# A transformer layer on one core: three top-k searches go from VectorE to ScalarE, one goes to a later stage, and tile start addresses are evened out

## The chip, the cores and the metric

The program runs on one core of a Trainium2 chip (trn2). The metric is device microseconds of one execution. A core has five instruction queues, each issued in order: TensorE (PE in the profile; its weight loads have a row of their own, PEld), VectorE (DVE), ScalarE (ACT), GpSimd (POOL) and SyncE (SP), which here only starts DMA transfers. All working data lie in SBUF, an on-chip memory with 128 partitions; matrix products go to PSUM. Tile sizes below are given as partitions x elements.

## The reference

One layer over 2048 tokens of width 1024, all in float32, then a final normalisation:

```
h   = RMSNorm(x);  P = h @ W_in              # split into conv inputs, q, k, v, iq, ik, iw, gates
y_a = (B * causal_conv3(C * x_a)) @ W_a
score[t,s] = sum_h iw[t,h] * relu(iq[t,h] . ik[s])    # causal, 8 index heads
keep the 256 best s of each t; softmax attention over these (8 heads, one k and v), bias by distance
y_b = attn @ W_b
x   = x + (sigmoid(g_a) * y_a + sigmoid(g_b) * y_b) @ W_out
x   = x + (silu(h2 @ W_g) * (h2 @ W_u)) @ W_d,   h2 = RMSNorm(x)
out = RMSNorm(x)
```

The choice of the 256 best must be exact, ties included. Queries are handled in 16 blocks of 128 (block 0 to 15). Blocks 0 and 1 have no more than 256 keys and need no choice, so a threshold is searched for in blocks 2 to 15. Block b has (b+1)*128 keys.

## The kernel before

**Arithmetic.** Each float32 product is made of three matmuls in the fp32r type: both operands are split into a rounded part (`hi`, written by ScalarE, line 129) and the rest (`lo`, line 130), and `mm3` (lines 155 to 157) multiplies hi by hi, hi by lo and lo by hi. A matmul has a stationary operand, 128x128, loaded ahead of it, and a moving operand of up to 512 columns.

**Stages.** The first stage forms all projections of h (lines 489 to 553). Between its matmuls, one in three, `proj` takes a step of `scores`: `score(b)` multiplies the index heads of a block with the keys (lines 258, 259, tile `sc`), ScalarE takes the relu (261, tile `r`), VectorE weights and sums (266, tile `acc`), and the finished scores go to memory (`SD`). When a block is scored, its threshold is searched. Then come two halves, each of eight blocks: attention (`attention(half)`, blocks 7 to 0, then 15 to 8), the mixer (branch products, gates, W_out, RMSNorm and transposes of h2), and the feed-forward layer (FFN, from line 889 on), with tiles `wgu` (gate and up weights), `h2hi`/`h2lo`, `hid` and `wd`. Half 0 attends to blocks 0 to 7 and needs their masks alone; half 1 needs those of blocks 8 to 15.

**The search.** Two versions give the same threshold. `descend(b)` on VectorE counts in each of 32 passes how many keys reach a trial value (line 285, tile `J`) and corrects the trial value by small instructions on 128x1 tiles (316 to 341). `descend_act(b)` makes integer keys on VectorE (381 to 384), then ScalarE does the 33 passes: a Sign over all keys with a running sum (358, tile `dump`, with a read of the accumulator), and two small instructions (367, 369, tiles `way` and `nt`). In the middle VectorE takes ScalarE's result (393, `top<-nt`) and makes new keys (400, 401); at the end it takes the second result (410, `li<-nt`). After either, `topk` (425 to 448) turns scores and threshold into a mask of 0 and -1e30 on VectorE and SP writes it to memory (`MS`). The tables `A_ACT`, `A_DVE` and `C_ACT` say which block is searched where: before, blocks 2, 3, 4 by VectorE and 5 to 10 by ScalarE in the first stage; 15, 14, 13, 12, 11 by ScalarE after half 0's attention, in its mixer and FFN. One search runs at a time, since the search tiles have one buffer each.

**What sets the order.** Each engine's queue is fixed when the program is built. A scheduler puts instructions into it by data dependencies, priority and its own estimate of when operands are ready; searches have the lowest priority (`tc.high_priority(offset=-LOW)`), so they fill what the scheduler takes for gaps. On the chip a queue goes in order: if an instruction waits, all behind it on that engine wait. `tc.issue_after(ins)` puts the instructions of its block that are on the engine of `ins` behind it in the queue (an order, not a wait). `ends[-1]` is VectorE's last `pl` of attention (line 680), `transposed[-1]` its last `h2lo` (line 150) of the mixer.

**Where tiles start.** SBUF is handed out in pools, from the left end or (`side="right"`) from the right end, one after the other, each tile rounded up to 32 bytes; so the size of a small tile shifts what lies beyond it. The built program gives these start addresses, modulo 512 bytes, of matmul operands before:

| product (output <- moving, stationary) | moving | stationary |
|---|---|---|
| first stage: `mm`, `sc` | 320 | 320 |
| attention logits `lg` | 320 | 320 |
| attention transposes `tpb<-ident,pr` | 128 | 192 |
| attention values `pv<-ph,V` and `pv<-pl,V` | 192 | 320 |
| mixer, `gu<-y,wab`, half 0 / half 1 | 320 / 448 | 320 / 448 |
| mixer, `gu<-o,wab`, half 0 / half 1 | 320 / 320 | 320 / 448 |
| W_out, `dn<-mg,o` | 320 | 320 |
| FFN gate and up, `gu<-h2,wgu`, half 0 / half 1 | 320 / 320 | 320 / 448 |
| FFN down, `dn<-hid,wd` | 320 | 320 |

Of the kernel before, what the change touches and what calls it, by code (L numbers as in the profile page):

```python
# [12 lines left out]
F32 = mybir.dt.float32  # L13
# [12 lines left out]
P = 128  # L26
# [4 lines left out]
CH = 512  # L31
# [15 lines left out]

A_ACT, A_DVE = (5, 6, 7, 8, 9, 10), (2, 3, 4)
C_ACT, C_DVE = (15, 14, 13, 12, 11), ()
ORDER = ((7, 6, 5, 4, 3, 2, 1, 0), (15, 14, 13, 12, 11, 10, 9, 8))  # L50
# [24 lines left out]
def trunk_kernel(tc, x, g_mix, w_in, b_gate, conv_w, w_a, w_b, w_out, rel_bias,  # L75
# [38 lines left out]
    bg = const.tile([P, 16], F32, name="bg")  # L114
    zero = edge.tile([P, 1], F32, name="zero")
    nc.gpsimd.memset(zero, 0.0)
# [133 lines left out]
    def score(b):  # L250
# [3 lines left out]
        for s0, w in cut((b + 1) * P):  # L254
            acc = tk.tile([P, CH], F32, name="acc", tag="acc", bufs=2)
            for h in range(NH):
                sc = scp.tile([P, CH], F32, name="sc", tag="sc")
                nc.tensor.matmul(sc[:, 0:w], iqb[:, h, :], IKH[:, s0:s0 + w], start=True, stop=False)
                nc.tensor.matmul(sc[:, 0:w], iqb[:, h, :], IKL[:, s0:s0 + w], start=False, stop=True)
                r = tk.tile([P, CH], F32, name="r", tag="r", bufs=3)  # L260
                nc.scalar.activation(r[:, 0:w], sc[:, 0:w], AF.Relu)  # L261
# [29 lines left out]
    def parts(b):  # L291

        for s0, w in cut((b + 1) * P):
            S = TK["p"].tile([P, CH], F32, name="S", tag="S", bufs=2)
            nc.sync.dma_start(out=S[:, 0:w], in_=SD[b][:, s0:s0 + w])
            yield slice(s0, s0 + w), w, S[:, 0:w].bitcast(U16).rearrange("p (n e) -> p n e", e=2)

# [155 lines left out]

    def select_block_act(b):
        with tc.high_priority(offset=-LOW):
            thr = descend_act(b)
            topk(b, thr, TK["a"].tile([P, TK["alen"]], U8, name="dump", tag="dump", bufs=1).bitcast(BF16))

# [100 lines left out]
    def attention(half):  # L559
# [3 lines left out]
        ap = pool(b_stack, f"ap{half}")  # L563
        prp = pool(b_stack, f"pr{half}")
        lgp = pool(b_stack, f"lg{half}", bufs=LGB, space=PSUM)
        tpb = pool(b_stack, f"tpb{half}", bufs=7 - LGB, space=PSUM)
# [47 lines left out]
        def logits(st, hg, res):  # L614

            b, n, q, Mt, spans, near, MBs = st
            lw = spans[-1][1]
            sums = ap.tile([P, 4], F32, name="sums", tag="sums", bufs=3)
            for hh in range(4):
# [3 lines left out]
                pr = prp.tile([P, LH], F32, name="pr", tag="pr", bufs=PRB[half])  # L623
                mx = ap.tile([P, 5], F32, name="mx", tag="mx", bufs=6)
                for i, (s0, w) in enumerate(spans):
# [12 lines left out]
                yield  # L638
            rec = ap.tile([P, 4], F32, name="rec", tag="rec", bufs=3)
            nc.vector.reciprocal(rec, sums)  # L640
            res.append(rec)

        def spread(b, hg, rec):

            tp = tpb.tile([P, CH], F32, name="tpb", tag="tpb")
            in_order(nc.tensor.transpose(tp[0:4, 0:P], rec, ident))
            row = ap.tile([4, P], F32, name="row", tag="row", bufs=2)
            nc.scalar.copy(row, tp[0:4, 0:P])
            rd = RD[2 * b + hg]
            nc.sync.dma_start(out=rd, in_=row)  # L650
            R = ap.tile([P, CH], F32, name="R", tag="R", bufs=3)
            nc.sync.dma_start(out=R, in_=bass.AP(rd[:].tensor, rd[:].offset, [[0, P], [1, CH]]))
            return R
# [90 lines left out]
    for half in (0, 1):  # L744
        ends = attention(half)
        mc = ExitStack()
        if half == 0:
            search_pool(mc, "tkc", C_DVE, C_ACT, 4)
            TK["p"].tile([P, 16], F32, name="pad")
        bigp = pool(mc, f"bigp{half}", bufs=4)  # L750
# [119 lines left out]
        if half == 0:  # L870
            with tc.issue_after(ends[-1].ins):
                for b, ba in itertools.zip_longest(C_DVE, C_ACT):
                    if ba is not None:
                        select_block_act(ba)
                    if b is not None:
                        select_block(b)
        if half == 1:
# [104 lines left out]
```

## Time and profile before

| | |
|---|---|
| median of 3 runs | 3313.43 us (3310.44 to 3317.68) |
| the profiled execution | 3308.23 us, span 3306.3 us |
| granted TensorE clock, mean | 0.99 |
| first stage | to about 1004 us |
| half 0: attention, mixer, FFN | to about 1140, 1360 and 2072 us |
| half 1: attention, mixer, FFN | to about 2390, 2576 and 3297 us |

The profile is of one execution. "x" is a count of instructions; a stretch "A:B" is in us from the start of the span. Recorded matmuls overlap, since their ends are modelled: a matmul of 512 columns is recorded with some 390 ns, while the next starts about 227 ns later, so for speed the count in a stretch says more than the mean duration. The number in brackets behind a row of the timeline is the time that the engine stood idle before it and what ended that.

### The profile page before, as it was taken

To read this page: it belongs to the slowest core of one execution; us is meant where nothing else is said; L and a number is where in the kernel's file an instruction comes from. 1 tells how busy PE (TensorE), PEld (TensorE's weight loads), DVE (VectorE), ACT (ScalarE), POOL (GpSimd) and SP (SyncE) were. 2 spreads that over 40 slices of the span, in tenths; PEclk is the share of its full clock that TensorE was granted. 3 is DMA by queue.
4 is the path that set the end of the run, shared out by engine and by line. 5 is a ranking of instruction groups with operands and counts; after the bars stand their busy time and mean duration, and the time that the engine had idled before them with its cause. 6 is when DMAs were issued, how large, how long until landed. Compare 5 with 4: busy or idle time off the path is not lost.

```text
span 3306.3 us, 41232 instructions
## 1 busy us (share of the span) xinstructions
PE 3206.5 (97%) x14723; PEld 2626.5 (79%) x14723; DVE 1744.3 (53%) x3422; ACT 1763.8 (53%) x3250; POOL 774.4 (23%) x684
## 2 busy tenths in 40 slices
PE   8999899999997899899999999999999999999999
PEld 6777788888886678788888888787787888888887
DVE  6389756565327775554535423898854422332234
ACT  6433478877877786867586611677632211111111
POOL 5411012221013520321221222222222222212221
PEclk9999999999999999999999999999999999999999
DMA  7643333333235692322212211422571411111111
GB/s 231 179 126 115 93 97 96 92 98 107 85 99 137 167 287 78 98 78 83 88 60 77 79 51 60 115 60 72 149 250 45 147 51 44 46 51 45 45 45 51
DMA packets 347077, 328.94 MB, mean 99 GB/s; under 512 B 20596, under 2 KB 276808, under 8 KB 346488
## 3 DMA queue, kind: packets, MB, share of 16 engines
q1 hardware_dynamic: 310248, 297.84, 29.4%
q0 software_dynamic: 36624, 28.48, 4.0%
q8 instruction: 115, 1.88, 0.2%
q14 instruction: 90, 0.74, 0.1%
HBM read 252.28 MB, written 75.54 MB: 99 GB/s over the span
## 4 chain that ended last, share of the span: by engine, by line
PE 79%; DVE 9%; DMA 5%; ACT 3%; issue 2%; POOL 1%; SPq 0%; POOLq 0%; DVEq 0%; ACTq 0%
PE gu L155 11%; PE gu L157 11%; PE gu L156 11%; PE mm L157 6%; PE mm L155 6%; PE mm L156 6%; PE dn L155 5%; PE dn L157 5%; PE dn L156 5%; PE tpb L676 3%; DVE J L285 2%; PE pv L663 2%; PE lg L629 1%; PE pv L664 1%; PE lg L630 1%
## 5 line engine op out<-in xcount | busy, mean ns | idle before, releaser
L155 PE MATMUL gu<-h2hi,wgu 128*128 128x512 f32 x1408 | 552.7, 393 | 0.0
L156 PE MATMUL gu<-h2lo,wgu 128*128 128x512 f32 x1408 | 552.1, 392 | 0.0
L157 PE MATMUL gu<-h2hi,wgu 128*128 128x512 f32 x1408 | 552.0, 392 | 0.0
L358 ACT ACTIVATE dump<-key,nt 128x768 uint8<-128x768 int16 (+21 forms) x330 | 484.2, 1467 | 8.4
L157 PE MATMUL mm<-hThi,wlo 128*128 128x512 f32 (+2 forms) x1216 | 471.7, 389 | 2.6 <-POOL wlo L130 2.5
L155 PE MATMUL mm<-hThi,whi 128*128 128x512 f32 (+2 forms) x1216 | 473.7, 390 | 0.4 <-ACT whi L129 0.4
L156 PE MATMUL mm<-hTlo,whi 128*128 128x512 f32 (+2 forms) x1216 | 471.1, 388 | 0.0
L937 DVE SCALAR_TENSOR_TENSOR x<-dn,x 128x512 f32<-128x512 f32 x352 | 241.7, 689 | 224.4 <-PE dn L157 224.3
L130 POOL TENSOR_TENSOR wlo<-raw,whi 128x512 fp32r<-128x512 f32 (+1 forms) x132 | 175.9, 1333 | 696.8 <-ACT whi L129 659.3
L156 PEld LDWEIGHTS gu<-h2lo,wgu 128*128 128x128 f32 x1408 | 265.2, 188 | 58.5
L157 PEld LDWEIGHTS gu<-h2hi,wgu 128*128 128x128 f32 x1408 | 265.0, 188 | 58.6
L155 PEld LDWEIGHTS gu<-h2hi,wgu 128*128 128x128 f32 x1408 | 265.2, 188 | 58.4
L130 POOL TENSOR_TENSOR hid<-th,hid 128x512 fp32r<-128x512 f32 x88 | 114.6, 1302 | 808.1 <-ACT hid L129 800.8
L266 DVE SCALAR_TENSOR_TENSOR acc<-r,iwT,acc 128x512 f32<-128x512 f32 (+2 forms) x266 | 196.1, 737 | 197.3 <-ACT r L261 196.6
L920 DVE SCALAR_TENSOR_TENSOR th<-th,gu 128x512 f32<-128x512 f32 x88 | 60.5, 687 | 432.5 <-ACT th L919 379.0
L130 POOL TENSOR_TENSOR wgu<-raw,wgu 128x1024 fp32r<-128x1024 f32 x88 | 216.6, 2462 | 271.5 <-ACT wgu L129 268.4
L155 PE MATMUL dn<-wd,hid 128*128 128x512 f32 x704 | 274.5, 390 | 0.0
L157 PE MATMUL dn<-wd,hid 128*128 128x512 f32 x704 | 274.1, 390 | 0.0
L156 PE MATMUL dn<-wd,hid 128*128 128x512 f32 x704 | 274.0, 389 | 0.0
L157 PEld LDWEIGHTS mm<-hThi,wlo 128*128 128x128 f32 (+1 forms) x1216 | 227.1, 187 | 54.5 <-POOL wlo L130 5.1
L155 PEld LDWEIGHTS mm<-hThi,whi 128*128 128x128 f32 (+1 forms) x1216 | 227.4, 187 | 44.1 <-ACT whi L129 1.7
L156 PEld LDWEIGHTS mm<-hTlo,whi 128*128 128x128 f32 (+1 forms) x1216 | 227.4, 187 | 42.9
(229 smaller groups left out, 5853.3 us busy)
## 6 DMA issues: line engine op xcount, KB each, us to landing
raw<-in_w_in_dram SPq DMA_DIRECT2D x124, 256.0 KB
raw<-in_w_ffn_gate_dram SPq DMA_DIRECT2D x44, 512.0 KB
raw<-in_w_ffn_up_dram SPq DMA_DIRECT2D x44, 512.0 KB
raw<-in_w_ffn_down_dram SPq DMA_DIRECT2D x44, 512.0 KB
S<-SD SPq DMA_DIRECT2D x80, 256.0 KB
GT<-f SPq DMA_DIRECT2D x64, 256.0 KB
ta<-GT SPq DMA_DIRECT2D x64, 256.0 KB
S<-SD SPq DMA_DIRECT2D x68, 192.0 KB
```

What stands on the lines that cost most here:

```text
L130: lo_eng.tensor_tensor(lo, raw, hi.bitcast(F32), op=ALU.subtract)
L155: nc.tensor.matmul(ps, whi, xhi, start=start, stop=False)
L156: nc.tensor.matmul(ps, whi, xlo, start=False, stop=False)
L157: nc.tensor.matmul(ps, wlo, xhi, start=False, stop=stop)
L266: nc.vector.scalar_tensor_tensor(acc[:, 0:w], r[:, 0:w], wv, acc[:, 0:w], op0=ALU.mult, op1=ALU.add)
L285: nc.vector.tensor_scalar(wide("J")[:, 0:n], xs, thr, None, op0=op, op1=ALU.add, accum_out=cnt)
L358: nc.scalar.activation(dump, keys, AF.Sign, bias=nt, accum_out=sm)
L629: in_order(nc.tensor.matmul(lg[:, o2:e2], q[:, h, :], KH[:, s0 + o2:s0 + e2], start=True, stop=False))
L663: in_order(nc.tensor.matmul(pv, V[:, sb, :], ph, start=sb == 0, stop=False))
L676: in_order(nc.tensor.transpose(tp[:, hh * P:(hh + 1) * P], Ps[hh][:, sb * P:(sb + 1) * P], ident))
L920: nc.vector.scalar_tensor_tensor(th, th, 1.0, g, op0=ALU.add, op1=ALU.mult)
L937: nc.vector.scalar_tensor_tensor(x2[tt][:, ns], ps, 0.5, x2[tt][:, ns], op0=ALU.mult, op1=ALU.add)
```

## The change

Four things are altered. Blocks 2 to 9 are searched by ScalarE in the first stage and none by VectorE; blocks 15 to 10 by ScalarE after half 0's attention, so block 10 moves from the first stage to there. Of these, only block 15's passes may start in the mixer: its `topk`, and all that VectorE does for blocks 14 to 10, is queued behind the last `h2lo`. Some buffers grow: `r` from 3 to 4, `S` (scores read back) from 2 to 4 in the second group. And tile sizes are set so that pools start elsewhere: `zero` takes 160 bytes instead of 4, the pad in the second search pool 448 instead of 64, and four small attention tiles go to a pool of their own (`few`).

```
-A_ACT, A_DVE = (5, 6, 7, 8, 9, 10), (2, 3, 4)
-C_ACT, C_DVE = (15, 14, 13, 12, 11), ()
+A_ACT, A_DVE = tuple(range(2, 10)), ()
+C_ACT, C_DVE = (15, 14, 13, 12, 11, 10), ()
...
-    zero = edge.tile([P, 1], F32, name="zero")
+    zero = edge.tile([P, 40], F32, name="zero")[:, 0:1]
...
-                r = tk.tile([P, CH], F32, name="r", tag="r", bufs=3)
+                r = tk.tile([P, CH], F32, name="r", tag="r", bufs=4)
...
-            S = TK["p"].tile([P, CH], F32, name="S", tag="S", bufs=2)
+            S = TK["p"].tile([P, CH], F32, name="S", tag="S", bufs=TK["eqs"])
...
-    def select_block_act(b):
-        with tc.high_priority(offset=-LOW):
+    def select_block_act(b, after=()):
+        with tc.high_priority(offset=-LOW), ExitStack() as stack:
             thr = descend_act(b)
+            for ins in after:
+                stack.enter_context(tc.issue_after(ins))
             topk(b, thr, TK["a"].tile([P, TK["alen"]], U8, name="dump", tag="dump", bufs=1).bitcast(BF16))
...
         prp = pool(b_stack, f"pr{half}")
+        few = pool(b_stack, f"few{half}")
...
-            sums = ap.tile([P, 4], F32, name="sums", tag="sums", bufs=3)
+            sums = few.tile([P, 4], F32, name="sums", tag="sums", bufs=3)
...
-            TK["p"].tile([P, 16], F32, name="pad")
+            TK["p"].tile([P, 112], F32, name="pad")
...
             with tc.issue_after(ends[-1].ins):
-                for b, ba in itertools.zip_longest(C_DVE, C_ACT):
-                    if ba is not None:
-                        select_block_act(ba)
-                    if b is not None:
-                        select_block(b)
+                select_block_act(C_ACT[0], [transposed[-1].ins])
+            with tc.issue_after(transposed[-1].ins):
+                for b in C_ACT[1:]:
+                    select_block_act(b)
```

The tiles `mx`, `rec` and `row` move to `few` in the same way as `sums`. In the built program after the change every operand of the table above starts at 320 modulo 512, but for `ident`, which stays at 128; the transposes so have 128 and 320.

The change moves instructions in the queues. Three places, all on VectorE, follow, each as it stood and as it stands now (line numbers past 297 are up to three higher after the change).

In the first stage, where block 2's search begins. `acc<-r` is the summing of scores, `f<-mm` (line 228) takes a projection out of PSUM, `J` is a counting pass. Before:

```order
L266 SCALAR_TENSOR_TENSOR acc<-r,iwT,acc 128x512
L316 TENSOR_SCALAR drop<-cnt 128x1
L318 SCALAR_TENSOR_TENSOR c<-c,drop 128x1
L228 SCALAR_TENSOR_TENSOR f_2222<-mm,f_2222 64x512
L285 TENSOR_SCALAR J,cnt<-up,c 128x384
L316 TENSOR_SCALAR drop<-cnt 128x1
L318 SCALAR_TENSOR_TENSOR c<-c,drop 128x1
L266 SCALAR_TENSOR_TENSOR acc<-r,iwT,acc 128x512
```

After:

```order
L266 SCALAR_TENSOR_TENSOR acc<-r,iwT,acc 128x512
L381 TENSOR_SCALAR key<-S 128x384
L382 TENSOR_SCALAR dump<-S 128x384
L384 SCALAR_TENSOR_TENSOR key<-dump,key 128x384
L266 SCALAR_TENSOR_TENSOR acc<-r,iwT,acc 128x512
L228 SCALAR_TENSOR_TENSOR f_2197<-mm,f_2197 64x512
L266 SCALAR_TENSOR_TENSOR acc<-r,iwT,acc 128x512
L228 SCALAR_TENSOR_TENSOR f_2201<-mm,f_2201 64x512
```

The counting passes and their small instructions are gone from VectorE; three instructions that make the keys stand there once.

At the opening of half 0's attention. `pr,mx<-lg` (line 632, 635 after the change) takes logits out of PSUM; the profile calls it CUSTOM_DVE_ANT_0. Before:

```order
L401 SCALAR_TENSOR_TENSOR key<-S,base,dump 128x384
L410 TENSOR_SCALAR li<-nt 128x1
L413 TENSOR_TENSOR li<-li,turn 128x1
L415 TENSOR_TENSOR thr<-li,top 128x1
L425 SCALAR_TENSOR_TENSOR dump,cnt_7133<-S,thr,zerob 128x512 x2
L632 ISA pr,mx<-lg,Mt 128x512
L632 ISA mx 128x1
L431 TENSOR_TENSOR more<-cnt_7133 128x1
L632 ISA pr,mx<-lg,Mt 128x512
```

After:

```order
L446 SCALAR_TENSOR_TENSOR eq<-S,thr,eq 128x384
L447 TENSOR_SCALAR eq<-eq 128x384
L635 ISA pr,mx<-lg,Mt 128x512
L635 ISA mx 128x1
L635 ISA pr,mx<-lg,Mt 128x512
L635 ISA mx 128x1
L635 ISA pr,mx<-lg,MB,mx 128x512
```

Before, the end of block 10's search and its `topk` stand ahead of and among the first logits; now the first stage's last search, of block 9, ends ahead of them with its `topk`, and no search instruction stands among them.

At the end of half 0's mixer. `x<-dn` adds a W_out product, `o<-x` is the norm, `h2lo` the rest of a transposed tile that the FFN reads. Before:

```order
L150 TENSOR_TENSOR h2lo<-gu,h2hi 128x4x128
L381 TENSOR_SCALAR key<-S 128x512
L382 TENSOR_SCALAR dump<-S 128x512
L150 TENSOR_TENSOR h2lo<-gu,h2hi 128x4x128
L381 TENSOR_SCALAR key<-S 128x512
L384 SCALAR_TENSOR_TENSOR key<-dump,key 128x512
L140 SCALAR_TENSOR_TENSOR o_13632<-x_12890,rs,gB 128x1024
L382 TENSOR_SCALAR dump<-S 128x512
L381 TENSOR_SCALAR key<-S 128x384
L864 SCALAR_TENSOR_TENSOR x_12988<-dn,x_12988 128x512
```

After:

```order
L150 TENSOR_TENSOR h2lo<-gu,h2hi 128x4x128 x2
L140 SCALAR_TENSOR_TENSOR o_13264<-x_12522,rs,gB 128x1024
L867 SCALAR_TENSOR_TENSOR x_12620<-dn,x_12620 128x512
L150 TENSOR_TENSOR h2lo<-gu,h2hi 128x4x128 x2
L140 SCALAR_TENSOR_TENSOR o_13286<-x_12571,rs,gB 128x1024
L140 SCALAR_TENSOR_TENSOR o_13308<-x_12620,rs,gB 128x1024
L867 SCALAR_TENSOR_TENSOR x_12669<-dn,x_12669 128x512
L150 TENSOR_TENSOR h2lo<-gu,h2hi 128x4x128 x2
L140 SCALAR_TENSOR_TENSOR o_13330<-x_12669,rs,gB 128x1024
L150 TENSOR_TENSOR h2lo<-gu,h2hi 128x4x128 x8
L425 SCALAR_TENSOR_TENSOR dump,cnt_13610<-S,thr,zerob 128x512
```

Before, the key making of block 14 stands among the norms and transposes; now the search's next VectorE work, block 15's `topk`, stands behind the last `h2lo`.

More of the change, by code (lines that the diff above doesn't have):

```diff
@@ L623, in logits @@
                 pr = prp.tile([P, LH], F32, name="pr", tag="pr", bufs=PRB[half])
-                mx = ap.tile([P, 5], F32, name="mx", tag="mx", bufs=6)
+                mx = few.tile([P, 5], F32, name="mx", tag="mx", bufs=6)
                 for i, (s0, w) in enumerate(spans):
@@ L638, in logits @@
                 yield
-            rec = ap.tile([P, 4], F32, name="rec", tag="rec", bufs=3)
+            rec = few.tile([P, 4], F32, name="rec", tag="rec", bufs=3)
             nc.vector.reciprocal(rec, sums)
@@ L646, in spread @@
             in_order(nc.tensor.transpose(tp[0:4, 0:P], rec, ident))
-            row = ap.tile([4, P], F32, name="row", tag="row", bufs=2)
+            row = few.tile([4, P], F32, name="row", tag="row", bufs=2)
             nc.scalar.copy(row, tp[0:4, 0:P])
```

## The prediction

> **What bounds the kernel now.** I read the page first, then a table of stretches, then the waits and the timeline of the stretches that lose time. The page's busy line and its chain of waits:
>
> ```profile
> PE 3206.5 (97%) x14723; PEld 2626.5 (79%) x14723; DVE 1744.3 (53%) x3422; ACT 1763.8 (53%) x3250; POOL 774.4 (23%) x684
> ...
> PE 79%; DVE 9%; DMA 5%; ACT 3%; issue 2%; POOL 1%; SPq 0%; POOLq 0%; DVEq 0%; ACTq 0%
> ```
>
> TensorE sets the end. No matmul is removed, so time can come from two sources only: PE's idle stretches, and the pace of its matmuls. Busy time by stretch (length, busy us and count of each engine, granted clock, DMA) shows both:
>
> ```profile
> core 0: us, PE busy (x) PEld busy (x) DVE busy (x) ACT busy (x) POOL busy (x), PEclk, DMA share, GB/s
> 180.00:400.00 220.00, 204.42 (x890) 163.84 (x889) 198.53 (x583) 75.92 (x154) 26.00 (x21) 0.98 0.40 116
> 400.00:1004.00 604.00, 603.38 (x2694) 502.58 (x2694) 298.32 (x555) 496.79 (x1111) 105.75 (x88) 1.00 0.35 100
> 404.00:465.00 61.00, 61.00 (x278) 51.20 (x277) 21.67 (x43) 57.54 (x148) 8.75 (x7) 1.00 0.29 82
> ...
> 1004.00:1052.00 48.00, 32.21 (x153) 22.74 (x151) 38.30 (x101) 32.69 (x60) 15.56 (x22) 0.89 0.39 108
> ...
> 1320.00:1360.00 40.00, 30.23 (x149) 25.10 (x148) 32.94 (x48) 25.88 (x45) 13.84 (x15) 0.83 0.47 146
> 1400.00:2040.00 640.00, 640.00 (x2825) 529.90 (x2824) 278.39 (x500) 364.22 (x603) 143.01 (x77) 1.00 0.22 68
> 1890.00:2070.00 180.00, 180.00 (x795) 149.03 (x795) 53.89 (x77) 26.74 (x36) 44.17 (x31) 1.00 0.21 67
> 2072.00:2110.00 38.00, 35.81 (x167) 24.68 (x167) 34.82 (x87) 24.03 (x32) 8.15 (x13) 1.00 0.59 144
> 2536.00:2576.00 40.00, 36.37 (x176) 30.05 (x175) 27.28 (x31) 22.50 (x38) 17.24 (x19) 0.91 0.40 127
> 2600.00:3240.00 640.00, 640.00 (x2771) 521.07 (x2770) 187.73 (x259) 106.43 (x139) 142.76 (x82) 1.00 0.16 50
> ```
>
> Three stretches lose time while a search is on: 180:400 (VectorE 90% busy), 1004:1052 and 1320:1360. For the last two, half 1 has the same stage without a search (2072:2110, 2536:2576). And the two FFNs, the same 3168 matmuls each, run at different paces with PE busy throughout.
>
> **180:400, VectorE's own searches go.** What they cost VectorE there by group, and then, from the waits (us, times, longest), what PE waited for:
>
> ```profile
> L285 DVE TENSOR_SCALAR_CACHE_REDUCE J<-up,l 128x384 bf16<-128x384 uint16 (+2 forms) x48 | 35.8, 745 | 1.4
> L285 DVE TENSOR_SCALAR_CACHE_REDUCE J<-up,c 128x384 bf16<-128x384 bf16 (+2 forms) x45 | 33.5, 745 | 1.3
> L341 DVE SCALAR_TENSOR_TENSOR l<-l,ldrop 128x1 f32<-128x1 f32 x48 | 11.3, 235 | 1.4
> ```
>
> ```profile
> PE sc L258 <- ACT r L261: 13.2, 11, 6.5
> ```
>
> The counts and the three other small groups beside L341 (each of 45 to 48 instructions) took roughly 100 us of VectorE. With them gone the sums of scores no longer queue, `r` comes free and ScalarE can empty `sc`, which is what PE waited for. The loss by count: 400:1004 holds 2694 matmuls in 604 us, 0.2242 each, with a like mix; 890 would take 199.5, so 20.5 us are lost in 220. By PE's busy time it is 15.6, since a modelled end hides part of a gap.
>
> The searches move to ScalarE. One pass costs a Sign, a read and two small instructions:
>
> ```profile
> L358 ACT ACTIVATE dump<-key,nt 128x768 uint8<-128x768 int16 x15 | 14.0, 934 | 0.4
> L358 ACT ACTIVATE dump<-key,nt 128x1408 uint8<-128x1408 int16 x15 | 22.0, 1468 | 0.4
> L358 ACT ACTIVATE dump<-key,nt 128x2048 uint8<-128x2048 int16 x15 | 30.0, 1997 | 0.3
> L358 ACT ACTIVATION_READ_ACCUMULATOR dump<-key,nt 128x1 f32 x330 | 61.8, 187 | 0.0
> L367 ACT ACTIVATE way<-sm,over 128x1 f32<-128x1 f32 x176 | 50.7, 288 | 2.6
> L367 ACT ACTIVATE way<-sm 128x1 f32<-128x1 f32 x176 | 34.2, 195 | 2.1
> L369 ACT ACTIVATE nt<-way,nt 128x1 f32<-128x1 f32 x330 | 96.5, 292 | 8.2
> ```
>
> Block 5 (768 keys): 33 x (0.934 + 0.187) + 16 x (0.288 + 0.195) + 32 x 0.292 = 54 us. Block 10 (1408): 72. The slope is 3.5 us per 128 keys, so blocks 2, 3, 4 come to an estimated 44, 47 and 51: ScalarE gains 142 us in the first stage and loses block 10's 72 there. What hides it: 404:465 lies inside block 5's search and has ScalarE 94% busy, PE 100%, VectorE 36%. ScalarE's own work in 180:400 is 75.92/220, 35%, and the search takes the rest as it comes. I take 19 of the 20.5 us; below it could be 10, if the shorter, more frequent passes make `r` late, above 21.
>
> The eight searches still end in time: block 10's own 72 us, the longest of the six of before, were done at 1012.75 (below). Now the longest is block 9's, 128 keys shorter, the first can start as soon as block 2 is scored, and in the queue block 9's `topk` stands ahead of the first logits.
>
> **1004:1052, block 10 leaves.** The timeline:
>
> ```profile
> 1005.71 0.39 PE L630 MATMUL lg<-KL,q 128*128 128x512 f32 x1
> ...
> 1012.75 0.15 DVE L410 TENSOR_SCALAR li<-nt 128x1 int32<-128x1 f32 x1 [39.84 <-ACT nt L369]
> ...
> 1014.79 0.69 DVE L632 CUSTOM_DVE_ANT_0 pr<-lg,Mt 128x512 f32<-128x512 f32 x1
> ...
> 1015.54 0.80 PE L629 MATMUL lg<-KH,q 128*128 128x512 f32 x1 [9.44 <-DVE mx L632]
> ```
>
> VectorE's queue stood at L410 for ScalarE's last pass; the first L632 was behind it and three PSUM tiles were full. Then `topk` shared VectorE with the logits until 1052. PE idles 48 - 32.21 = 15.8; half 1's opening idles 38 - 35.81 = 2.2, so 2.8 in 48. Gain 13; by count, 153 matmuls at 2072:2110's 167 in 38 need 34.8 of 48, again 13. Bounds: 9.4, the one stall, and 15.8, all idle time.
>
> Block 10's 72 us go behind block 11. What hides them: in 1890:2070 ScalarE is busy 26.74 of 180 us. The passes of the kernel before by their line (first and last start, us), and the first mask load of half 1 in GpSimd's timeline:
>
> ```profile
> L358 ACT ACTIVATION_READ_ACCUMULATOR dump<-key,nt x330: 185/187/201, 396.0 to 1873.0; 128x1 f32 x165
> ```
>
> ```profile
> 2056.50 0.55 POOL L600 DMA_DIRECT2D Mt<-MS  x1
> ```
>
> The search ended at about 1873. An estimated 20 us of `topk` and 100 to 120 for block 10 (its 72 us among ScalarE's other work, 15% there, and waits for VectorE at two points) put its mask near 2010, and it is the sixth block of half 1. Nothing. Without that cover, half 1 would wait for the excess.
>
> **1320:1360, the mixer's end.** The wait there (us, times, longest), VectorE's queue, and the same wait in 2536:2576:
>
> ```profile
> PE gu L147 <- DVE h2lo L150: 9.8, 4, 5.6
> ```
>
> ```profile
> 1339.34 2.60 DVE L382 TENSOR_SCALAR dump<-S 128x512 bf16<-128x512 bf16 x1
> ...
> 1343.33 1.27 DVE L150 TENSOR_TENSOR h2lo<-gu,h2hi 128x512 fp32r<-128x512 f32 x2
> ```
>
> ```profile
> PE gu L147 <- DVE h2lo L150: 3.6, 4, 1.2
> ```
>
> Key making stood ahead of `h2lo`, and now does not. 9.8 against 3.6: 6 us, as 149 against 176 matmuls in 40 us say too (27 x 0.227). Bounds 2 and 7. What is late next: block 15's `topk` falls into the FFN's first 20 us. Four PSUM tiles hold PE's first 22 us of FFN output, so I price it at nothing.
>
> **A price.** Block 15's passes now begin after the mixer's second `wab` split, before after the seventh. Each is 2.0 us and what is behind it waits, while PE starts on few weights. I take 2 us; bounds 0 and 10 (five passes).
>
> **The addresses.** Per 512-column matmul, half 0's FFN takes 640/2825 = 226.5 ns, half 1's 640/2771 = 231.0. The groups in these two stretches, half 0 first:
>
> ```profile
> L155 PE MATMUL gu<-h2hi,wgu 128*128 128x512 f32 x622 | 242.0, 389 | 0.0
> L157 PE MATMUL dn<-wd,hid 128*128 128x512 f32 x320 | 124.5, 389 | 0.0
> ```
>
> ```profile
> L155 PE MATMUL gu<-h2hi,wgu 128*128 128x512 f32 x604 | 238.5, 395 | 0.0
> L157 PE MATMUL dn<-wd,hid 128*128 128x512 f32 x320 | 125.2, 391 | 0.0
> ```
>
> The product whose stationary operand starts at 448 and moving one at 320 is the slow one; `dn`, 320 and 320 in both, is nearly even. ScalarE, VectorE and DMA are all less busy in half 1, so neighbours do not explain it. With all at 320 half 1 should run at 226.5: 3168 x 4.5 ns = 14 us. Bounds 0 and 15 (a little in `gu<-o,wab`). In attention the transposes' `ident` stays at 128, so I expect nothing, at best 3 us.
>
> The Trainium skill says otherwise. Its page "TensorE: Matmul & The Clock Gate" (Part 2, Step-by-step) gives PE two independent read ports and states "Loading the next tile's weights doesn't steal SBUF read bandwidth from the running matmul". By that rule the start addresses change nothing and this term is 0. The two paces above speak against it, though they do not prove the cause.
>
> **Sum.** -19 - 13 - 6 + 2 - 14 = -50 on the profiled execution's 3308.2: 3258. The runs' median, 3313.4, lies 5 higher, and the result will be a median too: 3263. Its own range: -21 - 16 - 7 - 18 = -62 to -10 - 9 - 2 + 10 = -11, so 3251 to 3302.
>
> **Rivals.** *Addresses do nothing* (13%): 3263 + 14 = 3277. For it, half 1's FFN differs in other ways too, such as the final norms of half 0 that it carries; against it, gate and up differ and down hardly.
>
> *ScalarE takes VectorE's place as limit in 180:400* (10%): PE waits for `r` all the same, and the 19 us stay: 3282. For it, 94% busy in a search and more `f` evacuations at 180:400 than later; against it, 0.62 us idle in 604 beside six such searches.
>
> *VectorE's queue stands for ScalarE's results* (7%): what happened at 1012.75 repeats. There are now 16 such points in the first stage (393 and 410 for eight blocks), with `acc` and `f` behind them. Each that holds PE for 9.4 us takes that back; from the sixth on (56 us) the kernel is slower than before, 3319, with eight 3338. Against it: ten such points in 400:1004 cost PE 0.62 us together. That the change does not do what it says is ruled out by the queues and the start addresses shown.
>
> **How the numbers follow.** The forecast holds 65%, the rivals 30, a larger gain (attention too, or stalls of 1100:1160) 5. The time is 3263. 3242 to 3294 holds the forecast's own range but its end, the first two rivals and half of the larger gains. A measurement of this kernel tells some 0.2%, 7 us. Slower: the third rival, 7%. Within 0.2%: the second and first together with poor other terms, 5%. Faster: 88%.
>
> **What would show it.** Right: in the stretch after block 2 is scored, PE 99% busy and `PE sc <- ACT r` under 3 us; no L410 ahead of the first logits and PE idle under 5 us in their first 48; the same `gu <- h2lo` wait near 3.6; half 1's FFN at 226.5 ns a matmul. Wrong: 231 ns there (first rival); long idle times before L393 or L410 with PE idle at the same time (third); ScalarE at 99% with PE waiting for `r` (second).

## The result and the profile after

| | before | after |
|---|---|---|
| median | 3313.57 us (4 runs, 3310.44 to 3317.68) | 3264.53 us (4 runs, 3260.28 to 3265.59) |
| ratio | | 0.9849, 95% interval 0.9832 to 0.9866 |
| profiled execution, span | 3306.3 us | 3262.3 us |

The kernel became 49 us faster by the medians and 44.0 by the two profiled spans; 3263 was forecast. The page of after, its busy line and the shares of its chain:

```profile
PE 3184.9 (98%) x14723; PEld 2623.9 (80%) x14723; DVE 1667.0 (51%) x3046; ACT 1886.7 (58%) x3646; POOL 780.3 (24%) x684
...
PE 71%; ACT 11%; DMA 6%; DVE 6%; issue 4%; POOL 2%; SPq 0%; POOLq 0%; ACTq 0%; DVEq 0%
```

TensorE still sets the end; ScalarE's share of the chain has grown from 3 to 11%. The stretches of the prediction, at their new places (length, busy us and count of each engine, granted clock, DMA):

```profile
core 0: us, PE busy (x) PEld busy (x) DVE busy (x) ACT busy (x) POOL busy (x), PEclk, DMA share, GB/s
180.00:400.00 220.00, 220.00 (x999) 184.51 (x998) 96.37 (x192) 192.91 (x537) 27.70 (x23) 1.00 0.40 119
980.00:1028.00 48.00, 45.07 (x248) 34.95 (x247) 42.14 (x115) 38.92 (x76) 21.46 (x32) 1.00 0.38 104
...
1290.00:1330.00 40.00, 37.56 (x190) 30.72 (x189) 33.17 (x52) 18.80 (x31) 14.07 (x14) 1.00 0.37 116
1400.00:2030.00 630.00, 624.66 (x2742) 515.07 (x2742) 295.62 (x529) 425.76 (x724) 148.00 (x84) 1.00 0.25 76
...
2560.00:3200.00 640.00, 640.00 (x2825) 530.01 (x2824) 190.99 (x262) 107.92 (x142) 147.05 (x87) 1.00 0.18 54
```

First row: 999 matmuls where 890 stood, and PE never idle. Second: the 48 us around attention's opening have PE idle for 2.9 us instead of 15.8. In the second and third row the granted clock is 1.00, where it was 0.89 and 0.83. Last: 640/2825 = 226.5 ns a matmul in half 1's FFN. The row that nobody forecast is 1400:2030: in half 0's FFN PE, which had been without a gap, now idles 5.3 us, and 2742 matmuls stand where 630 us at 226.5 ns would hold 2781, 8.9 us fewer.

For the comparison of runs the program is cut by the starts of the first matmul of each stage in the trace (first `lg` of a half for attention, first `gu` from `wgu` for the FFN; the first stage begins with the program's first matmul, the last ends with its last). Lengths in us:

| stage | before | after | difference | forecast |
|---|---|---|---|---|
| first stage | 996.7 | 973.0 | -23.7 | -19 |
| half 0, attention and mixer | 353.4 | 330.7 | -22.7 | -13 - 6 + 2 = -17 |
| half 0, FFN | 707.5 | 718.5 | +11.0 | 0 |
| half 1, attention and mixer | 499.2 | 505.0 | +5.8 | 0 |
| half 1, FFN | 733.1 | 718.7 | -14.4 | -14 |
| sum | | | -44.0 | -50 |

The new loss shows in PE's waits in half 0's FFN of after (us, times, longest); before, this list is empty:

```profile
PE dn L155 <- ACT hid L129: 3.1, 2, 1.9
PE dn L157 <- POOL hid L130: 1.9, 3, 0.6
PE dn L155 <- DVE x L939: 0.9, 1, 0.9
PE dn L155 <- DVE base L397: 0.9, 1, 0.9
```

One of these places, followed back from PE. PE's timeline of after, then ScalarE's and VectorE's ahead of it:

```profile
1488.71 0.39 PE L157 MATMUL dn<-wd,hid 128*128 128x512 f32 x1
1490.96 0.50 PE L155 MATMUL dn<-wd,hid 128*128 128x512 f32 x1 [1.87 <-ACT hid L129]
```

```profile
1486.03 1.79 ACT L358 ACTIVATE dump<-key,nt 128x1792 uint8<-128x1792 int16 x1
...
1488.51 1.79 ACT L358 ACTIVATE dump<-key,nt 128x1792 uint8<-128x1792 int16 x1
...
1490.30 0.61 ACT L129 ACTIVATE hid<-th 128x512 fp32r<-128x512 f32 x1
```

```profile
1478.05 0.60 DVE L445 SCALAR_TENSOR_TENSOR eq<-cs,need,eq 128x384 bf16<-128x384 f16 x1
1478.57 0.68 DVE L923 TENSOR_TENSOR th<-gu,th 128x512 f32<-128x512 f32 x1
1479.17 0.68 DVE L384 SCALAR_TENSOR_TENSOR key<-dump,key 128x512 int16<-128x512 bf16 x1
...
1482.96 0.56 DVE L384 SCALAR_TENSOR_TENSOR key<-dump,key 128x384 int16<-128x384 bf16 x1
1483.44 0.68 DVE L922 SCALAR_TENSOR_TENSOR th<-th,gu 128x512 f32<-128x512 f32 x1
1484.22 0.69 DVE L923 TENSOR_TENSOR th<-gu,th 128x512 f32<-128x512 f32 x1
```

Block 14's `topk` and block 13's keys stand among the gate and up products: between the L923 of one 512-column unit and the L922 of the next VectorE ends that `topk` and makes keys for 4 us. The next unit's `th` is done at 1484.91, and then ScalarE has passes of block 13 (1792 keys) queued ahead of `hid`, which starts 5.4 us later. The down product needs that very `hid`. Before, block 14's `topk` stood among the down products, where its pieces lie between the `x` (L937) and no `th` waits:

```profile
1475.59 0.67 DVE L937 SCALAR_TENSOR_TENSOR x<-dn,x 128x512 f32<-128x512 f32 x1
1476.17 0.14 DVE L444 CAST last<-cs 128x1 f32<-128x1 f16 x1
1476.23 0.74 DVE L445 SCALAR_TENSOR_TENSOR eq<-cs,need,eq 128x512 bf16<-128x512 f16 x1
1476.89 0.48 DVE L441 TENSOR_SCALAR eq<-S,thr 128x512 bf16<-128x512 f32 x1
1477.28 0.74 DVE L446 SCALAR_TENSOR_TENSOR eq<-S,thr,eq 128x512 bf16<-128x512 f32 x1
1477.94 0.68 DVE L937 SCALAR_TENSOR_TENSOR x<-dn,x 128x512 f32<-128x512 f32 x1
```

### The profile page after: what moved, and what is told of

It is laid out like the page before. It is cut to its first block, busy times and chain, and to the rows that moved or that the text cites. A ratio compares the mean times of both kernels' runs of the same rounds, so it can differ in the third digit from the quotient of the medians.

```text
span 3262.3 us, 41287 instructions
## 1 busy us (share of the span) xinstructions
PE 3184.9 (98%) x14723; PEld 2623.9 (80%) x14723; DVE 1667.0 (51%) x3046; ACT 1886.7 (58%) x3646; POOL 780.3 (24%) x684
## 4 chain that ended last, share of the span: by engine, by line
PE 71%; ACT 11%; DMA 6%; DVE 6%; issue 4%; POOL 2%; SPq 0%; POOLq 0%; ACTq 0%; DVEq 0%
PE mm L155 8%; PE mm L157 8%; PE mm L156 8%; PE gu L157 7%; PE gu L155 7%; PE gu L156 7%; ACT dump L358 6%; PE dn L155 4%; PE dn L157 4%; PE dn L156 4%; PE tpb L679 3%; PE sc L259 2%; PE sc L258 2%; PE pv L666 2%; PE pv L667 2%
## 5 line engine op out<-in xcount | busy, mean ns | idle before, releaser
L358 ACT ACTIVATE dump<-key,nt 128x384 uint8<-128x384 int16 (+27 forms) x420 | 549.0, 1307 | 10.7
L922 DVE SCALAR_TENSOR_TENSOR th<-th,gu 128x512 f32<-128x512 f32 x88 | 60.3, 685 | 391.9 <-ACT th L921 355.2
```

The lines of the kernel that those rows point to most:

```text
L358: nc.scalar.activation(dump, keys, AF.Sign, bias=nt, accum_out=sm)
```

## The experiments

All stage lengths below are taken from the traces as in the table above. "before" in a comparison is the kernel before on the same chip.

| run | median us | first stage | half 0 att.+mixer | half 0 FFN | half 1 att.+mixer | half 1 FFN |
|---|---|---|---|---|---|---|
| before | 3313.57 | 996.7 | 353.4 | 707.5 | 499.2 | 733.1 |
| after | 3264.53 | 973.0 | 330.7 | 718.5 | 505.0 | 718.7 |
| e8_zero | 3307.67 | 995.9 | 351.6 | 722.5 | 502.3 | 719.6 |
| e9_addr | 3296.11 | 996.7 | 352.0 | 707.5 | 500.7 | 718.1 |
| e2_noaddr | 3274.51 | 972.0 | 331.1 | 717.7 | 504.4 | 733.4 |
| e6_apart_64 | 3280.98 (1 run) | 971.9 | 328.2 | 723.9 | 504.9 | 733.8 |
| e7_apart_256 | 3260.27 (1 run) | 972.1 | 329.4 | 716.9 | 504.2 | 719.4 |
| e12_ident | 3261.91 | 972.4 | 330.4 | 717.4 | 503.3 | 719.7 |
| e13_blocks_2_4 | 3312.39 | 973.0 | 377.0 | 708.5 | 502.4 | 733.0 |
| e4_nohold | 3270.24 | 972.1 | 333.0 | 724.5 | 502.1 | 718.9 |
| e3_two_S | 3275.62 | 972.8 | 330.4 | 732.6 | 502.8 | 718.2 |
| e10_two_S_nohold | 3261.76 | 971.8 | 343.8 | 708.4 | 501.0 | 718.5 |
| e11_late_keys | 3265.11 | 972.3 | 333.5 | 719.6 | 503.5 | 718.7 |
| e14_in_down | 3259.89 | 973.0 | 336.4 | 710.8 | 504.3 | 718.6 |

### Do the addresses do it? One size on the kernel before

```diff
-    zero = edge.tile([P, 1], F32, name="zero")
+    zero = edge.tile([P, 40], F32, name="zero")[:, 0:1]
```

> The kernel before with one size changed: `zero` takes 160 bytes. No instruction moves on any engine; the gate and up weights of half 0 now start at 192 modulo 512 and those of half 1 at 320 (before 320 and 448), their moving operand at 320 as ever. Theory (unlike start addresses slow a matmul): the paces change places, half 0's FFN goes from 226.5 to 231 ns a matmul, 707 to 721 us, half 1's from 231 to 226.5, 733 to 719 us; the total stays, 3313 within 4. Rival (half 1's FFN is slower by other work of its own, addresses do nothing): 707 and 733 us both stay.

Median 3307.67 us against 3311.13 of before, ratio 0.9991 (0.9982 to 1.0001). The paces changed places. The same two stretches of this run:

```profile
1400.00:2030.00 630.00, 630.00 (x2729) 513.16 (x2728) 276.90 (x496) 361.17 (x596) 137.26 (x74) 1.00 0.22 69
2600.00:3220.00 620.00, 620.00 (x2737) 513.39 (x2736) 181.22 (x249) 108.74 (x144) 149.62 (x89) 1.00 0.18 56
```

Half 0: 630/2729 = 230.9 ns; half 1: 620/2737 = 226.5. Nothing else in the FFNs differs from before, so the start address of the stationary operand sets the pace here, while the moving one stays at 320, and what half 1's FFN does besides (the final norms) does not.

The second run evens out both halves:

```diff
+    zero = edge.tile([P, 40], F32, name="zero")[:, 0:1]
...
+            TK["p"].tile([P, 112], F32, name="pad")
```

> The kernel before with `zero` of 160 bytes and the pad of 448: both halves' gate and up weights start at 320 modulo 512, no instruction moves on any engine. Theory: half 1's FFN takes 719 us and not 733, all else stays, 3313 - 14 = 3299. Rival (addresses do nothing): 733 us, 3313.

3296.11 us, ratio 0.9954 (0.9941 to 0.9966): 15.0 us less than before's 3311.13. In the trace half 1's FFN alone moved, 733.1 to 718.1. Rival "addresses do nothing" is refuted.

The complement, the changed kernel with the old sizes (`mx`, `rec` and `row` go back to `ap` like `sums`):

```diff
-    zero = edge.tile([P, 40], F32, name="zero")[:, 0:1]
+    zero = edge.tile([P, 1], F32, name="zero")
...
-            TK["p"].tile([P, 112], F32, name="pad")
+            TK["p"].tile([P, 16], F32, name="pad")
...
-            sums = few.tile([P, 4], F32, name="sums", tag="sums", bufs=3)
+            sums = ap.tile([P, 4], F32, name="sums", tag="sums", bufs=3)
```

> The changed kernel with the old sizes (`zero` 4 bytes, pad 64, no pool `few`): the search moves alone. The order differs from the changed kernel only at the end of half 0's attention and in its mixer's opening. Theory: half 1's FFN back at 733 us, 3264 + 14 = 3278; first stage 24 us shorter than before, half 0's attention to its FFN 23 shorter, its FFN 11 longer, as in the changed kernel. Rival (addresses do nothing, the 14 us came with the moved searches): 3264.

3274.51 us, ratio 0.9891 (0.9877 to 0.9904): 37 us less than before by the moved searches alone, and half 1's FFN back at 733.4. 37 and 15 add up to 52; the whole change gave 49. That half 0's FFN takes 717.7 here shows that its loss came with the searches and not with the sizes.

### How far apart?

The changed kernel, with no instruction moved, only the size of `zero`, first 64 bytes apart:

```diff
-    zero = edge.tile([P, 40], F32, name="zero")[:, 0:1]
+    zero = edge.tile([P, 24], F32, name="zero")[:, 0:1]
```

> The changed kernel with `zero` of 96 bytes: no instruction moves; the gate and up weights of both halves start at 384 modulo 512, their moving operand at 320: 64 bytes apart instead of 128 as in half 1 before. Theory (any unlike start modulo 512 slows the matmul): both FFNs at 231 ns a matmul, half 1's 733 us, half 0's 718 + 14 = 732, total 3293. Rival (64 apart is near enough): 3264.

Then 256 bytes apart:

```diff
-    zero = edge.tile([P, 40], F32, name="zero")[:, 0:1]
+    zero = edge.tile([P, 104], F32, name="zero")[:, 0:1]
```

> The changed kernel with `zero` of 416 bytes: no instruction moves; the gate and up weights of both halves start at 64 modulo 512, their moving operand at 320: 256 bytes apart. Theory (any unlike start modulo 512): both FFNs at 231 ns a matmul, 3293. Rival (what counts repeats every 256 bytes): 226.5 ns and 3264.

The half 1 stretch of the first, then of the second:

```profile
2600.00:3220.00 620.00, 620.00 (x2683) 503.68 (x2682) 176.65 (x244) 100.18 (x129) 133.60 (x73) 1.00 0.15 45
```

```profile
2600.00:3220.00 620.00, 620.00 (x2737) 513.39 (x2736) 176.14 (x244) 103.35 (x134) 137.81 (x76) 1.00 0.15 45
```

64 apart: 620/2683 = 231.1 ns, as slow as 128 apart. 256 apart: 226.5 ns, as fast as equal. My theory "any unlike start modulo 512" fell; these distances (0, 64, 128 either way, 256) fit something that repeats every 256 bytes, and the loss does not grow from 64 to 128.

In all of these FFNs the moving operand starts at 320, so they alone cannot say whether the distance counts or the place of the stationary operand by itself. The mixer of half 1 in the kernel before can: its two products share `wab`, which starts at 448, while `y` starts at 448 and `o` at 320. First and sixth of six matmuls in a row, of the one and of the other:

```profile
2399.79 0.39 PE L157 MATMUL gu<-y,wab 128*128 128x512 f32 x1
...
2400.92 0.40 PE L156 MATMUL gu<-y,wab 128*128 128x512 f32 x1
```

```profile
2424.61 0.39 PE L155 MATMUL gu<-o,wab 128*128 128x512 f32 x1
...
2425.77 0.40 PE L157 MATMUL gu<-o,wab 128*128 128x512 f32 x1
```

Five steps take 1.13 us with `y` and 1.16 with `o`. Over all such matmuls of that mixer that start less than 300 ns apart, the median step is 227 ns with `y` and 232 with `o`. With the same stationary operand the like start is the fast one, so the distance counts.

In the first of the two runs half 0's FFN took 723.9 us and not the expected 732; PE's idle time there shrank, as it would if slower matmuls leave VectorE and ScalarE more time. The half 0 stretch of that run:

```profile
1400.00:2030.00 630.00, 629.53 (x2719) 510.41 (x2719) 294.50 (x525) 425.64 (x722) 149.54 (x84) 1.00 0.24 74
```

0.5 us idle instead of 5.3: the two losses overlap and don't add.

The last operand that was left unlike is `ident`. It was allocated after other constants:

```diff
-    ident = const.tile([P, P], F32, name="ident")
     nhalf = const.tile([P, 1], F32, name="nhalf")
...
     vecT = const.tile([P, 28], F32, name="vecT")
+    zerob = const.tile([P, 1], BF16, name="zerob")
+    ident = const.tile([P, P], F32, name="ident")
     bg = const.tile([P, 16], F32, name="bg")
...
-    zerob = const.tile([P, 1], BF16, name="zerob")
```

> The changed kernel with `ident` allocated later in its pool, so that it starts at 320 modulo 512 instead of 128, like the `pr` that it transposes; no instruction moves. Theory (unlike starts disturb the transposes, and through them the 231 to 232 ns of the logits between them): attention 3 us shorter in each half (130 and 309 us), 3258. Rival (the transposes of 128 columns do not feel it, the waits for `pr` and `mx` set the pace): 3264.

3261.91 us, ratio 0.9853 (0.9838 to 0.9868), not told apart from the change's 0.9849. Attention took 130.4 and 308.8 us in the two halves, after 130.2 and 309.4. The rival holds: in attention the start of `ident` does not show.

### Are the first two gains separate?

The kernel before with blocks 2, 3 and 4 searched by ScalarE, and nothing else:

```diff
-A_ACT, A_DVE = (5, 6, 7, 8, 9, 10), (2, 3, 4)
+A_ACT, A_DVE = tuple(range(2, 11)), ()
```

> The kernel before with one part of the change alone: blocks 2, 3 and 4 searched by ScalarE, block 10 left in the first stage, old addresses, old buffers, no hold. Theory (the two gains are separate: VectorE's passes cost the first stage 23 us, block 10's end costs the opening of attention 14 to 17): first stage 973 us instead of 996.7, half 0's attention about 144 as before, total 3312 - 23 = 3289. Rival (it was block 10's leaving that made room in the first stage): first stage 985 us or more, 3300.

3312.39 us against 3311.64, ratio 1.0004 (0.9994 to 1.0013): nothing gained. The first stage did take 973.0 us, so the rival of that expectation is wrong too; but half 0's attention and mixer took 377.0 us instead of 353.4, and gave back all 23.6. VectorE's timeline where that attention begins:

```profile
981.72 0.69 DVE L632 CUSTOM_DVE_ANT_0 pr<-lg,Mt 128x512 f32<-128x512 f32 x1 [26.52 <-PE lg L630]
...
992.70 0.15 DVE L393 TENSOR_SCALAR top<-nt 128x1 f32<-128x1 f32 x1 [10.28 <-ACT nt L369]
...
993.65 0.69 DVE L632 CUSTOM_DVE_ANT_0 pr<-lg,Mt 128x512 f32<-128x512 f32 x1
```

And PE's waits, and the engines in 1004:1052, of the same run:

```profile
PE pv L663 <- ACT t L668: 18.8, 11, 4.0
PE lg L629 <- DVE mx L632: 17.6, 6, 11.2
PE gu L156 <- DVE y L130: 9.1, 1, 9.1
```

```profile
1004.00:1052.00 48.00, 43.32 (x262) 36.03 (x261) 40.93 (x110) 48.00 (x104) 18.54 (x26) 1.00 0.31 74
```

The first stage ends earlier and block 10's search does not: it is still half done when attention begins. VectorE stands 10.3 us at L393 for ScalarE's `nt` with the logits behind it, which is the third rival's mechanism, one stage later. That stand costs no more than the one at L410 before: attention's 150th matmul comes 46.7 us after its first, before 48.0. The 23.6 us are lost behind it. The second half of the search keeps ScalarE busy for all of 1004:1052, and PE waits 18.8 us for its `t`, against 4.6 before; at the mixer's opening PE waits 9.1 us for a `y` that stands in VectorE's queue behind block 10's `topk`. The fourth `r` buffer is not what shortens the first stage, since this run has three and the same 973.0. So the 23.7 us of the first stage are worth something only because block 10 leaves it.

### What does half 0's FFN lose, and why?

First reading: amount (six searches and block 15's last part) or place (the hold behind the last `h2lo`). The hold taken out:

```diff
-                select_block_act(C_ACT[0], [transposed[-1].ins])
-            with tc.issue_after(transposed[-1].ins):
-                for b in C_ACT[1:]:
+                for b in C_ACT:
                     select_block_act(b)
```

> The changed kernel without the second wait in the queue: all six late searches stand only behind the last `pl`, so block 15's `topk` and block 14's key making may stand in the mixer again. Theory (half 0's FFN lost 11 us by place: `topk` and the next keys stand ahead of the third `hid` unit of a pair, which the down product reads first; without the hold they stand ahead of the first and fourth): that FFN 707 to 711 us instead of 718.5, the mixer's end loses some 10 again by `h2lo`, total 3264 within 5. Rival (the FFN lost 11 us by amount: a sixth search and block 15's last part on VectorE and ScalarE): the FFN stays at 718 or so and the mixer's 10 come back on top, 3274.

3270.24 us, ratio 0.9880 (0.9867 to 0.9894), slower than the change. The FFN took 724.5 us, more than with the hold, and attention with mixer 333.0, so the mixer's end lost only 2.3 and not 10. Neither theory as written; PE now waits mostly for `x`, the sum that empties `dn`:

```profile
PE dn L155 <- DVE x L937: 7.7, 6, 3.2
```

Second reading: the buffers `S`, which the change raises from 2 to 4 there and which let the scheduler bunch search work. With the hold, and without:

```diff
-            S = TK["p"].tile([P, CH], F32, name="S", tag="S", bufs=TK["eqs"])
+            S = TK["p"].tile([P, CH], F32, name="S", tag="S", bufs=2)
```

> The changed kernel with two buffers `S` instead of four in the second search group; the hold behind the last `h2lo` stays. Without the hold (the run before) half 0's FFN lost not less but more, 17.9 us, and there PE waited for `x`, which empties `dn`, 7.7 us: so the place ahead of one unit or another is not the cause. New theory (bunching: four buffers let the scheduler put many pieces of `topk` and of the next keys together, ahead of `th` or `x`; two spread them out between the `x`): half 0's FFN loses under 4 us instead of 11.8, 3264 - 8 = 3256. Rival (the hold's place: in this kernel too search work stands ahead of the second and third unit of the pairs): FFN 718 us, 3264.

> The changed kernel with two buffers `S` and without the hold: half 0's late searches stand as in the kernel before, but for block 10, which stands behind block 11. Theory (bunching by the four buffers): half 0's FFN 707 to 710 us as before the change, the mixer's end waits for `h2lo` again (9.5 us before, 4.6 without the hold), total 3264 - 9 + 5 = 3260. Rival (the amount, a sixth search, costs the FFN 11 us and more): FFN 718 us or more, 3270.

With the hold: 3275.62 us, ratio 0.9896 (0.9880 to 0.9913), the FFN 732.6, the worst of all:

```profile
PE dn L155 <- ACT hid L129: 13.7, 4, 6.3
```

Without: 3261.76 us, ratio 0.9849 (0.9834 to 0.9864), the FFN 708.4, with six searches in it, and no wait of PE in it at all; the mixer's end waits for `h2lo` again:

```profile
PE gu L147 <- DVE h2lo L150: 9.6, 4, 6.0
```

So amount is refuted (the sixth search costs 0.9 us, 708.4 against 707.5). Bunching by four buffers does not explain it either: two made the FFN shorter without the hold (708.4 against 724.5) and longer with it (732.6 against 718.5). What is left is the place. A pair of the FFN (two column tiles each of gate and up, then their down products) takes some 64 us (707.5 over 11 pairs), with 8 `th` and then 16 `x` in VectorE's queue; a search takes about two pairs, so a place, once taken, comes back at every second pair. Where block 14's `topk` begins in the queue, and how long that FFN took:

| run | place of block 14's `topk` | FFN, us |
|---|---|---|
| before | behind 7 of 8 `th`, ahead of the first `x`; later ones at `x` 7 to 9 | 707.5 |
| e10_two_S_nohold | behind 6 `th`; later ones at `x` 4 to 8, the last ahead of the first | 708.4 |
| after | at the last `x`, next keys behind 2 and 3 `th` | 718.5 |
| e3_two_S | behind 1 `th` of the next pair, next keys behind 4 | 732.6 |
| e4_nohold | behind 5 `th`, the next two behind 5 and 3 | 724.5 |

Two tries to put it among the down products and keep the hold, both with two buffers `S`. The first writes blocks 14 to 10 after the FFN's first pair, behind its last `th`:

```diff
-            with tc.issue_after(transposed[-1].ins):
-                for b in C_ACT[1:]:
-                    select_block_act(b)
...
-                    nc.vector.tensor_tensor(th, u, th, op=ALU.mult)
+                    last_th = nc.vector.tensor_tensor(th, u, th, op=ALU.mult)
...
+            if half == 0 and fpair == 0:
+                with tc.issue_after(last_th.ins):
+                    for b in C_ACT[1:]:
+                        select_block_act(b)
```

> The changed kernel with two buffers `S`, and all VectorE work of blocks 14 to 10 behind the last `th` of the FFN's first pair instead of the last `h2lo` (they are written after that pair; block 15 is held as in the change). Reading so far: what half 0's FFN loses depends on where `topk` and the next keys fall in the 66 us of a pair (between the gate and up products, where `hid` or `x` behind them comes late, or in the stretch of down products, where nothing urgent is behind them), and a search takes about two pairs, so a bad place repeats (26.0 us lost with the hold and two buffers, 1.7 without the hold). Theory: moved on by half a pair they fall among the down products again; the FFN loses under 4 us and the mixer's end keeps its gain: 3264 - 9 = 3255. Rival (any hold costs the FFN, since block 10's search then falls late): FFN 718 us or more, 3264 or more.

3265.11 us, ratio 0.9861 (0.9845 to 0.9878), the FFN 719.6: missed. Its `topk` of blocks 14 to 11 begin behind 5, 6, 6 and 6 `th` of their pairs, and PE waits for `x` 7.1 us. The second moves it on by six `x`:

```diff
-                    nc.vector.scalar_tensor_tensor(x2[tt][:, ns], ps, 0.5, x2[tt][:, ns], op0=ALU.mult, op1=ALU.add)
+                    down = nc.vector.scalar_tensor_tensor(x2[tt][:, ns], ps, 0.5, x2[tt][:, ns], op0=ALU.mult, op1=ALU.add)
+                    if half == 0 and fpair == 0 and 2 * tt + n == 5:
+                        held = down
+            if half == 0 and fpair == 0:
+                with tc.issue_after(held.ins):
+                    for b in C_ACT[1:]:
+                        select_block_act(b)
```

> The changed kernel with two buffers `S`, and all VectorE work of blocks 14 to 10 behind the sixth `x` of the FFN's first pair (tt 2, second half). Reading of the seven orders run so far, by where a block's `topk` begins in VectorE's queue within a pair (8 `th`, then 16 `x`): from the end of the last `th` to the tenth `x`, half 0's FFN lost 1.7 us (before, and two buffers without hold); behind one to four `th` of the next pair, or with the next keys there, 12 to 26; ahead of the last two or three `th`, 13 to 18, also when the hold was moved by half a pair. Here every `topk` begins between the second and the eleventh `x`, the last one behind the last `th`. Theory (place in the queue decides): the FFN 707 to 711 us, the mixer's end as in the changed kernel, total 3264 - 9 = 3255 (3252 to 3259). Rival (any hold costs the FFN, whatever the place): FFN 717 us or more, 3262 or more.

The FFN took 710.8 us. PE's waits in it and at the mixer's end:

```profile
PE gu L147 <- DVE h2lo L150: 2.7, 3, 1.2
PE dn L155 <- DVE x L936: 1.6, 3, 0.8
PE dn L157 <- POOL hid L130: 0.6, 1, 0.6
PE dn L155 <- ACT hid L129: 0.6, 1, 0.6
```

Its `topk` of blocks 14 to 11 begin behind the second, tenth, tenth and eighth `x`, block 10's behind 7 of 8 `th`. So the loss goes with the place, and a hold with other places costs the FFN 3.3 us at most. The whole came to 3259.89 us and not 3255, ratio 0.9841 (0.9828 to 0.9855), which the intervals don't tell apart from the change: attention and mixer of half 0 took 336.4 us here and 330.7 in the change. The two buffers alone are not the reason, since e3_two_S has them too and took 330.4; why the new order costs 5.7 us there was not tried. One place keeps its exception: the first `topk` of e10_two_S_nohold stands behind 6 `th` as in e11_late_keys and did no harm, so "behind 5 or 6 `th`" is what went with the loss, not a proven rule. Only one place, in the trace of after, was followed from VectorE to PE.

## Why the prediction was right, and where it was wrong

**180:400, -19: measured -22.7.** Counted at equal matmuls, the 1800th starts 22.7 us earlier, a little past the bound of 21; 890 matmuls in the stretch became 999. Of the three sizes offered (20.5 by count, 15.6 by busy time, 19 taken) the one by count came nearest, and the cause was named rightly: `sc` no longer waits for `r`, also with three buffers `r` (973.0 in e13_blocks_2_4). What was called its cover held as well: PE is busy throughout while ScalarE is 192.91/220 = 88% busy, so the second rival did not come.

**1004:1052, -13: measured -17.5**, outside its bounds of 9.4 to 15.8. The 150th matmul of attention comes 30.5 us after the first instead of 48.0. The bounds took only PE's idle time, of which 14.4 us went (15.8 to 1.4). The term left out is the granted clock. Before, it was 0.50 behind the stall of 9.44 us:

```profile
1015.54:1020.40 4.86, 4.86 (x11) 3.34 (x12) 4.04 (x14) 2.58 (x5) 1.97 (x3) 0.50 0.26 83
```

These 11 matmuls start some 0.43 us apart, those from 1020.60 on, at 1.00, 0.23 apart: an estimated 2.3 us more, from these two paces. The prediction's own row had 0.89 in its clock column and did not use it. A second step failed too: the sum added the first term to this one as if the first could be had alone. e13_blocks_2_4 shows that it could not; whether the second could was not tried.

**The mixer, -6 and +2: measured about -10.0 and +4.4.** From the 1400th matmul of half 0's attention and mixer to the FFN it takes 14.4 us instead of 24.4, past the bound of 7. The wait for `h2lo` fell from 9.8 to 2.3 us, below half 1's 3.6, and the granted clock over that end rose from 0.72 to 1.00. Between the 600th and the 1400th, from the end of attention through the mixer's opening, 4.4 us are lost, within the bounds of 0 and 10; how much of it block 15's passes cost is not separated.

**The addresses, -14: measured -14.4 in the whole change, -15.0 alone.** The term and its cause were right: unlike start addresses. Modulo 512, as the tables count, was too wide, since 256 bytes apart costs nothing. Attention was rightly priced at nothing. The rule of the Trainium skill that was weighed there ("TensorE: Matmul & The Clock Gate", Part 2, Step-by-step: two independent read ports) gives no difference between e8_zero's two halves; the runs show 230.9 against 226.5 ns with nothing but a start address changed, and the measurement decides. Why an address matters the runs do not show.

**Half 0's FFN, 0: measured +11.0.** This is the step that was mis-sized: "Four PSUM tiles hold PE's first 22 us of FFN output, so I price it at nothing", and "Nothing" for block 10 behind block 11. The second holds for the amount of work (0.9 us in e10_two_S_nohold). The first looked at block 15's `topk` alone and at the first 20 us. What the runs showed in its place: the hold and the four buffers `S` moved the starting point of a chain of six searches, each about two pairs long, and with it the place of every later `topk` and key making: ahead of `th` and `hid`, in every second pair. The order listings show the new place of block 15's `topk`; where the later ones would fall was never worked out. The prediction's question at 1320:1360, what is late next, was asked of the first `topk` only.

**Half 1's attention, 0: measured +5.8.** In half 1's attention and mixer the runs lie between 500.7 and 505.0, before at 499.2, and the change's address part is not the cause (504.4 without it). Counted at equal matmuls, 3.6 of the 5.8 us are lost in the first 150. That part goes with the four buffers `S`: with two and nothing else altered it is 0.5 (e3_two_S), and without the hold 2.9 with four and 0.0 with two (e4_nohold, e10_two_S_nohold). The one exception among the runs with two is e14_in_down, 4.8, where block 10's `topk` runs on into that attention. How the buffers reach it, and the rest of the loss, stay open.

**Third rival, 7%.** VectorE does stand for ScalarE at L410, and 27.75 us for block 9's last result, in after's timeline:

```profile
934.12 0.15 DVE L410 TENSOR_SCALAR li<-nt 128x1 int32<-128x1 f32 x1 [27.75 <-ACT nt L369]
```

PE was idle for none of it: behind it stood only that block's `topk`, and the first logits came at 981.53. In e13_blocks_2_4 the logits stood right behind, and PE waited 11.2 us. Its chance was set by how often such stands had been harmless; what decides is what is queued behind them at that point, and that can be read from the order.

That the total came within 2 us of the forecast is luck, since errors of both signs met: 4.7 us and 5.7 us more gain in the first two stages, 11.0 and 5.8 us of loss that had been priced at nothing, and medians that lie 49 us apart where the two profiled spans lie 44.

## What to carry to other kernels

When background work fills another engine's gaps in a fixed queue, ask where in the foreground's cycle each piece lands: the same six searches cost a stage between 0.9 and 25 us in the orders tried here, and if a piece lasts a whole number of cycles a bad place repeats. Before adding up the gains of a change's parts, ask of each whether the next stage can take it: a stage that ends 24 us earlier gains nothing while a search in its background runs on into the next. Read the granted clock beside the idle time: a stall can cost more than it lasts. And where two like stages run at different paces with the same engine busy throughout, compare the operands' start addresses.

## What the runs showed of the hardware

In the FFN a matmul of 512 columns (fp32r) started every 226.5 ns when the start addresses of its two operands were equal or 256 bytes apart, and every 231 ns when they were 64 or 128 bytes apart (averages over the FFN's mix, where only two matmuls in three are concerned). It was to be seen in one and the same program with one tile's size changed, and in one mixer with the same stationary operand (227 against 232 ns).

Behind a stall of PE the granted clock was seen at 0.50: in the trace of before, 11 matmuls behind 9.44 us of idle time started some 0.43 us apart, and 0.23 apart from 1020.60 on.

VectorE's 16-bit work was seen to stretch while GpSimd worked. Two pairs of rows of after, VectorE's, then GpSimd's:

```profile
1464.09 3.41 DVE L442 TENSOR_TENSOR_SCAN cs<-eq,last 128x512 f16<-128x512 bf16 x1
...
1471.30 1.28 DVE L442 TENSOR_TENSOR_SCAN cs<-eq,last 128x512 f16<-128x512 bf16 x1
```

```profile
1463.59 2.83 POOL L130 TENSOR_TENSOR wgu<-raw,wgu 128x1024 fp32r<-128x1024 f32 x1
1467.66 2.39 POOL L130 TENSOR_TENSOR wgu<-raw,wgu 128x1024 fp32r<-128x1024 f32 x1 [1.24 <-ACT wgu L129]
```

The same scan took 3.41 us beside GpSimd's weight split and 1.28 us when GpSimd was idle. This was read from one trace and not tried by itself.
